# A Conformer layer's shifted copies in another layout, and two modulation vectors made elsewhere

## The chip, the cores and the metric

The kernel runs on one NeuronCore of a Trainium2 chip. TensorE (PE in the profile) multiplies matrices into PSUM, VectorE (DVE) and ScalarE (ACT) work elementwise, GpSimd (POOL) and SyncE (SP) mostly issue DMAs, and 16 DMA engines serve the queues of the core. The metric is the device time of one execution in microseconds (us), the median over runs; lower is better.

## The reference

A backbone of four layers works on 256 latent tokens and 256 context tokens of width 1024, all in float32. Layers 0 and 3 mix tokens by attention, layer 1 by a Conformer convolution, layer 2 by a short convolution; each is followed by an MLP. Six modulation vectors for each layer (shift, scale and gate of the mixer, numbers 0 to 2, and of the MLP, 3 to 5) come from one product of a conditioning vector with `mod_w`, 1024 by 6144 for each layer.

```python
def conformer_conv(h, w1, b1, dw, dwb, ln_g, ln_b, w2, b2):
    a, g = jnp.split(h @ w1 + b1, 2, axis=-1)
    u = a * jax.nn.sigmoid(g)
    u = dwconv(u, dw) + dwb                      # 31 taps along the tokens, each channel by itself
    return jax.nn.silu(layernorm(u, ln_g, ln_b)) @ w2 + b2

mod_l = (silu_c @ mod_w[i] + mod_b[i]).reshape(b, N_MOD, 1, D_MODEL)      # mod_c the same, from c_ctx
x = x + mod_l[:, 2] * mixer(modulate(rmsnorm(x), mod_l[:, 0], mod_l[:, 1]))
x = x + mod_l[:, 5] * sq_relu_mlp(modulate(rmsnorm(x), mod_l[:, 3], mod_l[:, 4]))
```

## The kernel before

Channels lie on the 128 partitions, in eight tiles; both streams, latent and context, lie side by side along a tile, 512 columns. The big products split each float32 operand into a high and a low part and add three products (lines 105 to 107). A weight chunk comes by an SP load into one of four `raw` buffers, ScalarE rounds it (line 221), VectorE takes the rest (line 222), and the two parts fill two of ten `w` buffers. `gemm_turns` goes over a pair of chunks once for the latent stream and once more for the context stream, and holds the eight `w` buffers of the pair until the second turn is through.

A scheduler that is not part of the kernel orders the instructions of each engine, except that from the second group of the Conformer's first product on, TensorE keeps program order until the block `with in_order` ends. The SP queue works in order too: a DMA that waits holds up all behind it.

The Conformer (`conformer`) makes the gated product `glu` in four groups of two tiles. Tiles 0 and 1 are convolved on VectorE (`conv_vector`), tiles 2 to 7 on TensorE (`conv_tensor`): 31 taps are eight products, each of which takes four neighbouring taps at once, from copies that hold each of 32 channels four times on the partitions, shifted by 0, 8, 16 and 24 columns. `shifted` writes a tile's `glu` to DRAM (`mem`) and reads it back in four such copies (`u4`, shown as `u<-mem`). The first of the four shifts fills partitions 0 to 31, the second 32 to 63, and so on. Groups 1 and 2 (tiles 2 to 5) treat both streams at once, group 3 (tiles 6 and 7) one at a time. After group 3 TensorE runs `conv_tensor` of tiles 4 to 7 for the latent stream, the mean of the layer norm (`total` and four `conv` against `ones_d`, line 1044), the context half of tiles 4 and 5, sums of squares (line 490), tile 6, the spread of the result over the partitions (line 527), tile 7, and the context mean. Then come the context sums and spread, and the product with `cv_w2` (`project`), whose operand `z` is ready by stream.

A modulation vector is made in one of two ways. `mod_tensor` loads its 4 MB in eight `raw` buffers and uses TensorE (16 products, line 371, and four small ones, line 380). `mod_vectors` loads 256 KB pieces into four buffers of their own (`mraw`) and uses VectorE (lines 312 and 316, then 322 and 323). Both are generators, put in a list by `background`; `tick`, called at steps of the big products, advances the first one at the rate given, and `need` runs the list at once until a vector is there.

Layer 1's vectors 0 to 3 are made by `mod_vectors` in layer 0's MLP, 4 and 5 by `mod_tensor` at rate 0, so that `self.need(layer, 4, 5)` at the end of the block `with in_order` runs both there, on TensorE between the context mean and the context sums.

Of the kernel before, what the change touches and what calls it, by code (L numbers as in the profile page):

```python
# [8 lines left out]
F32 = mybir.dt.float32  # L9
# [16 lines left out]
CONF_K = 31  # L26
CONF_PAD = 15
PITCH = 288
VECTOR_TILES = (0, 1)
NEG = -1e30  # L30


class Net:
# [864 lines left out]
    def conv_taps(self, slot):  # L898


        nc = self.nc
        dw = self.t["cv_dw"][slot]
        src = self.tmp([P, 2, P])
        nc.gpsimd.memset(src[96:, 1, 96:], 0.0)
        for b in range(2):
            for i in range(4):
                n = 3 if 4 * b + i == 7 else 4
                nc.gpsimd.dma_start(out=src[32 * i:32 * i + 32, b, :32 * n], in_=bass.AP(
                    dw.tensor, dw.offset + (4 * b + i) * D, [[32, 32], [8 * D, n], [1, 32]]))
        yield  # L910
        taps = self.work.tile([P, 8, 32], F32, tag="acc", bufs=1, name=self.name("taps"))
        ps = self.ps("x")
        for b in range(2):
            nc.tensor.transpose(out=ps[:, b * P:(b + 1) * P], in_=src[:, b], identity=self.ident)
        nc.vector.tensor_copy(out=taps, in_=ps[:, :2 * P].rearrange("p (i q) -> p i q", q=32))
        yield taps, self.mask32

    def conformer(self, layer, slot, then):
        nc, t = self.nc, self.t
# [3 lines left out]
        conv = [None] * KT  # L923
        sig = {}
        two = lambda ap: ap.rearrange("p (s n) -> p s n", s=2)
# [26 lines left out]
                        [P, 4, 4, 32]), op=ALU.mult)  # L952
            return halves

        def shifted(j, st):


            if j not in u4:
                u4[j] = [self.work.tile([P, 2, LAT + 8], F32, tag="h", bufs=22, name=self.name("u4")) for _ in range(4)]
                mem[j] = self.dram.tile([P, 2, PITCH], F32, tag=f"mem{j}", name=self.name("mem"))  # L960
            nc.sync.dma_start(out=mem[j][:, st], in_=glu[j][:, st])
            n = len(range(2)[st])
            for q in range(4):
                src = mem[j][32 * q:32 * q + 32, st]
                nc.sync.dma_start(out=u4[j][q][:, st, :LAT + 7], in_=bass.AP(
                    src.tensor, src.offset, [[8, 4], [2 * PITCH, 32], [PITCH, n], [1, LAT + 7]]))

        def conv_tensor(j, st):

            n = len(range(2)[st]) * LAT  # L970
            ps = self.ps()
            out = ps[:, :n].rearrange("p (s n) -> p s n", n=LAT)
            for i in range(8):
                for q in range(4):
                    nc.tensor.matmul(out=out[32 * q:32 * q + 32], lhsT=tapw[j][i // 4][:, i % 4, q],  # L975
                                     rhs=u4[j][q][:, st, i:i + LAT], start=i == 0, stop=i == 7, tile_position=(0, 32 * q))
            nc.scalar.activation(out=two(conv[j])[:, st], in_=out, func=AF.Identity, bias=self.par("cv_dwb", j))
# [9 lines left out]
        u4, tapw, mem = {}, {}, {}  # L987
        glu = {}
        for g in range(4):
            def out(d, src, c, g=g):  # L990
                j = 2 * g + d % 2
                if d < 2:
                    if j not in sig:
                        sig[j] = self.tmp()
                    nc.scalar.activation(out=sig[j][:, c], in_=src, func=AF.Sigmoid, bias=self.par("cv_b1", KT + j))
                    return
                if j not in glu:
                    glu[j] = self.padded(j, CONF_PAD)
                for s in range(c.start // LAT, c.stop // LAT):
                    o = s * LAT - c.start  # L1000
                    nc.vector.scalar_tensor_tensor(out=glu[j][:, s, CONF_PAD:CONF_PAD + LAT], in0=src[:, o:o + LAT],
                                                   scalar=self.par("cv_b1", j), in1=sig[j][:, s * LAT:(s + 1) * LAT],
                                                   op0=ALU.add, op1=ALU.mult)
                if j not in VECTOR_TILES:
                    shifted(j, slice(c.start // LAT, c.stop // LAT))
                elif c.stop == NTOK:
                    conv[j] = self.hid()
                    on_vector.append(conv_vector(j, glu[j]))
                    next(on_vector[-1])
            segs = [(D + g * LAT, LAT), (g * LAT, LAT)]  # L1010
            if g == 0:
                self.gemm_turns(self.chunk_pair(w1, segs), acts, out, first=True)
                in_order.enter_context(self.tc.manual_schedule(engines={mybir.EngineType.PE}))
            elif g < 3:
                for i, _ in enumerate(self.gemm(w1, segs, acts, cols, out)):
                    run_some(3)
                    if g == 1 and i == 1:
                        taps, mask = next(loaded)
                    if g == 2 and i in (2, 4):
                        tapw[1 + i // 2] = tap_weights(1 + i // 2)  # L1020
            else:
                for j in (2, 3):
                    conv[j] = self.hid()
                    conv_tensor(j, slice(0, 2))
                self.gemm_turns(self.chunk_pair(w1, segs), acts, out)
                for j in (4, 5, 6, 7):
                    tapw[j] = tap_weights(j)
# [31 lines left out]

        with in_order:  # L1060
            for j in (4, 5, 6, 7):
                conv_tensor(j, slice(0, 1))
            lat = layer_norm(0)
            next(lat)
            for j in (4, 5):
                conv_tensor(j, slice(1, 2))
            next(lat)
            conv_tensor(6, slice(1, 2))
            next(lat)
            conv_tensor(7, slice(1, 2))  # L1070
            other = layer_norm(1)
            next(other)
            self.need(layer, 4, 5)
        for _ in other:
            pass
        self.need(layer, 2)
# [194 lines left out]
    def run(self, out):  # L1271
        self.begin()
        for m in (2, 3, 4, 5):
            self.background(self.mod_tensor, 0, [m], 0.5)
        self.credit = -1.0
        both, lat = (0, NTOK), (0, LAT)
        for layer in range(DEPTH):
            slot = layer // 3
            live = both if layer < DEPTH - 1 else lat
            mixer_end = lambda s, layer=layer: self.norm(layer, 1, s)  # L1280
            if layer == DEPTH - 1:
                mixer_end = self.last_norm
            if layer % 3 == 0:
                self.attention(layer, slot, live, mixer_end)
            elif layer == 1:
                self.conformer(layer, slot, mixer_end)
            else:
                self.short_conv(layer, slot, mixer_end)
            if layer < DEPTH - 1:
                for vectors, rate in (([0, 1], 0.55), ([2, 3], 0.55)) if layer == 0 else (([0, 1], 0.42), ([2], 0.42), ([3, 4], 0.42),  # L1290
                                                                                   ([5], 0.25)):
                    self.background(self.mod_vectors, layer + 1, vectors, rate)
                if layer == 0:
                    for m in (4, 5):
                        self.background(self.mod_tensor, 1, [m], 0.0)

                def layer_end(s, layer=layer):
                    self.norm(layer + 1, 0, s)
                self.mlp(layer, live, layer_end)
            else:  # L1300
                self.mlp(layer, live, lambda s: None)
        self.end(out)
# [35 lines left out]
```

## Time and profile before

| | |
|---|---|
| median of 3 runs | 2233.25 us (2231.36 to 2234.01) |
| profiled execution, its own time | 2232.96 us |
| its span, first to last instruction | 2231.2 us |
| TensorE busy in the span | 2188.0 us, 98% |
| VectorE busy | 1522.8 us, 68% |
| ScalarE busy | 865.7 us, 39% |
| mean granted clock of TensorE | 0.99 |

The rows further down come from the profiled execution. Times count from the start of the span. A granted clock of 1.00 is 2.4 GHz, 0.50 is 1.2 GHz, and a value between the two is a mean over a stretch that had both. A float32 product of the convolution or of the modulation stands as two records, one of the big products as one, and a few per cent of the records are missing.

### The profile page before, as it was taken

To read this page: it belongs to the slowest core of one execution; us is meant where nothing else is said; L and a number is where in the kernel's file an instruction comes from. 1 tells how busy PE (TensorE), PEld (TensorE's weight loads), DVE (VectorE), ACT (ScalarE), POOL (GpSimd) and SP (SyncE) were. 2 spreads that over 40 slices of the span, in tenths; PEclk is the share of its full clock that TensorE was granted. 3 is DMA by queue.
4 is the path that set the end of the run, shared out by engine and by line. 5 is a ranking of instruction groups with operands and counts; after the bars stand their busy time and mean duration, and the time that the engine had idled before them with its cause. 6 is when DMAs were issued, how large, how long until landed. Compare 5 with 4: busy or idle time off the path is not lost.

```text
span 2231.2 us, 32928 instructions
## 1 busy us (share of the span) xinstructions
PE 2188.0 (98%) x12804; PEld 1792.8 (80%) x12804; DVE 1522.8 (68%) x2656; ACT 865.7 (39%) x1453; POOL 94.7 (4%) x167
## 2 busy tenths in 40 slices
PE   8999999999999988999999999999999999999998
PEld 5767678888889664988888898898888888778998
DVE  5366568979546835697766886579757566688665
ACT  4355545232234104542232332242323244666543
POOL 1112100000000000000000000000000000230000
PEclk9999999999999998999999999999999999999999
DMA  9555545646332336254545544226455426455553
GB/s 317 149 94 93 128 121 166 192 139 193 99 98 88 104 119 214 92 161 146 167 135 166 170 133 132 95 81 208 146 170 185 145 68 188 69 82 156 191 186 124
DMA packets 203132, 318.57 MB, mean 143 GB/s; under 512 B 13957, under 2 KB 70209, under 8 KB 202976
## 3 DMA queue, kind: packets, MB, share of 16 engines
q1 hardware_dynamic: 199056, 309.75, 43.6%
q0 software_dynamic: 3616, 6.60, 4.9%
q8 instruction: 100, 1.64, 0.3%
q14 instruction: 56, 0.46, 0.1%
q10 hardware_dynamic: 304, 0.12, 0.0%
HBM read 313.60 MB, written 2.82 MB: 142 GB/s over the span
## 4 chain that ended last, share of the span: by engine, by line
PE 91%; DMA 4%; DVE 3%; issue 1%; ACT 1%; POOL 0%; SPq 0%; ACTq 0%; POOLq 0%; DVEq 0%
PE mm L105 27%; PE mm L107 27%; PE mm L106 27%; PE mm L745 2%; PE x L735 2%; DMA u<-mem 2%; PE mm L707 1%; PE mm L975 1%; PE x L371 1%; PE mm L706 1%; DMA e<-in_na_rpb_dram 1%; DMA raw<-in_mod_w_dram 0%; DVE w L222 0%; DMA raw<-in_mlp_w_dram 0%; PE x L270 0%
## 5 line engine op out<-in xcount | busy, mean ns | idle before, releaser
L221 ACT ACTIVATE w<-raw 128x1024 fp32r<-128x1024 f32 (+1 forms) x377 | 392.2, 1054 | 652.8 <-PE mm L106 559.2
L222 DVE TENSOR_TENSOR w<-raw,w 128x1024 fp32r<-128x1024 f32 (+1 forms) x377 | 454.3, 1221 | 270.5 <-ACT w L221 267.4
L105 PE MATMUL mm<-a,w 128*128 128x512 f32 (+2 forms) x1792 | 629.8, 352 | 2.3 <-DVE t L629 1.4
L106 PE MATMUL mm<-a,w 128*128 128x512 f32 (+2 forms) x1792 | 627.4, 351 | 0.0
L107 PE MATMUL mm<-a,w 128*128 128x512 f32 (+2 forms) x1792 | 625.0, 350 | 0.3 <-DVE w L222 0.3
L106 PE MATMUL mm<-h,w 128*128 128x256 f32 (+1 forms) x1504 | 507.3, 337 | 0.1
L105 PE MATMUL mm<-h,w 128*128 128x512 f32 (+1 forms) x1376 | 472.7, 344 | 0.1
L107 PE MATMUL mm<-h,w 128*128 128x512 f32 (+1 forms) x1376 | 471.1, 342 | 0.0
L105 PEld LDWEIGHTS mm<-a,w 128*128 128x128 f32 x1792 | 337.5, 189 | 53.3 <-issue 5.7
L107 PEld LDWEIGHTS mm<-a,w 128*128 128x128 f32 x1792 | 337.9, 189 | 48.0 <-DVE w L222 0.9
L106 PEld LDWEIGHTS mm<-a,w 128*128 128x128 f32 x1792 | 338.5, 189 | 45.5
L106 PEld LDWEIGHTS mm<-h,w 128*128 128x128 f32 x1504 | 284.4, 189 | 32.3 <-DVE h L222 0.5
L105 PEld LDWEIGHTS mm<-h,w 128*128 128x128 f32 x1376 | 259.3, 188 | 36.2 <-issue 3.9
L107 PEld LDWEIGHTS mm<-h,w 128*128 128x128 f32 x1376 | 259.1, 188 | 32.6 <-DVE mm L713 0.6
L316 DVE SCALAR_TENSOR_TENSOR macc<-mraw,cw,macc 128x512 f32<-128x512 f32 x392 | 272.7, 750 | 11.1 <-DMA mraw<-in_mod_w_dram 10.3
L588 DVE SCALAR_TENSOR_TENSOR x<-mm,mod,x 128x256 f32<-128x256 f32 x288 | 127.6, 480 | 93.4 <-PE mm L107 92.6
L221 ACT ACTIVATE h<-t 128x512 fp32r<-128x512 f32 (+1 forms) x148 | 80.7, 546 | 105.9 <-DVE t L619 89.3
L222 DVE TENSOR_TENSOR h<-t,h 128x512 fp32r<-128x512 f32 (+1 forms) x148 | 86.4, 585 | 28.9 <-ACT h L221 28.8
L618 ACT ACTIVATE t<-mm 128x512 f32<-128x512 f32 (+1 forms) x136 | 69.0, 509 | 94.0 <-PE mm L107 92.7
L619 DVE SCALAR_TENSOR_TENSOR t<-mm,t 128x512 f32<-128x512 f32 (+1 forms) x136 | 79.5, 587 | 37.1 <-ACT t L618 36.7
L556 ACT ACTIVATE a<-t,mod 128x256 fp32r<-128x256 f32 x120 | 53.4, 500 | 58.9 <-DVE t L543 58.9
L723 ACT ACTIVATE t<-mm,s 128x512 f32<-128x512 f32 (+1 forms) x96 | 58.9, 616 | 44.0 <-DVE s L721 43.2
(172 smaller groups left out, 1805.3 us busy)
## 6 DMA issues: line engine op xcount, KB each, us to landing
raw<-in_mlp_w_dram SPq DMA_DIRECT2D x256, 512.0 KB
mraw<-in_mod_w_dram SPq DMA_DIRECT2D x256, 256.0 KB
raw<-in_mod_w_dram SPq DMA_DIRECT2D x48, 512.0 KB
raw<-in_na_wqkv_dram SPq DMA_DIRECT2D x64, 256.0 KB
raw<-in_sc_win_dram SPq DMA_DIRECT2D x24, 512.0 KB
h<-in_mod_w_dram SPq DMA_DIRECT2D x32, 256.0 KB
raw<-in_na_wqkv_dram SPq DMA_DIRECT2D x16, 512.0 KB
raw<-in_na_wo_dram SPq DMA_DIRECT2D x16, 512.0 KB
```

The lines of the kernel that those rows point to most:

```text
L105: mm(out=out, lhsT=a[0], rhs=b[0], start=start, stop=False)
L106: mm(out=out, lhsT=a[0], rhs=b[1], start=False, stop=False)
L107: mm(out=out, lhsT=a[1], rhs=b[0], start=False, stop=stop)
L221: self.nc.scalar.activation(out=hi, in_=src, func=AF.Copy)
L222: self.nc.vector.tensor_tensor(out=lo, in0=src, in1=hi.bitcast(F32), op=ALU.subtract)
L316: nc.vector.scalar_tensor_tensor(out=acc[s], in0=raw, scalar=c, in1=acc[s], op0=ALU.mult, op1=ALU.add)
L556: self.nc.scalar.activation(out=hi[:, c], in_=t, func=AF.Identity, bias=sh)
L588: self.nc.vector.scalar_tensor_tensor(out=x, in0=src[:, o:o + LAT], scalar=self.mod1(layer, m, s, j), in1=x, op0=ALU.mult, op1=ALU.add)
L618: nc.scalar.activation(out=r, in_=src, func=AF.Relu)
L619: nc.vector.scalar_tensor_tensor(out=h, in0=src, scalar=0.0, in1=r, op0=ALU.max, op1=ALU.mult)
L723: nc.scalar.activation(out=soft[:, g], in_=s[:, g], func=AF.Exp, bias=nm[:, i:i + 1], accum_out=sm[:, i:i + 1])
L735: nc.tensor.transpose(out=tp[:, dst * P:(dst + 1) * P], in_=p[:, j * P:(j + 1) * P], identity=self.ident)
```

## The change

Four parts.

- The four shifts of a channel lie on neighbouring partitions (partition 4c + s instead of 32s + c), so that the read back from DRAM goes over 32 channels, then four shifts, then columns. The taps are put in the same order by one ScalarE copy ahead of their transpose, and the mask that picks them comes from one VectorE reduction instead of the constant `mask32`.
- For tiles with both streams (2 to 5), the streams lie in DRAM in one run, the left padding of the second being the right padding of the first, so that each partition reads one run of 534 columns instead of two of 263. It is written by two DMAs instead of one. Tiles 6 and 7 get a DRAM buffer for each stream instead of halves of one.
- `conv_tensor` takes one stream at a time everywhere: for tiles 2 and 3 that is 64 products of 256 columns each instead of 32 of 512.
- Layer 1's vector 4 is made by `mod_vectors` in layer 0's MLP (all at rate 0.5 there instead of 0.55), and vector 5 by `mod_tensor` at rate 0.45 in layer 1's own MLP. `self.need(layer, 4, 5)` goes.

```diff
+CLOSE = CONF_PAD + 256
...
+        turned = self.tmp([P, 2, P])
+        nc.scalar.copy(out=turned.rearrange("p b (c s) -> p b s c", s=4), in_=src.rearrange("p b (s c) -> p b s c", s=4))
...
+        mask = self.work.tile([P, 32], F32, tag="red", bufs=1, name=self.name("mask"))
+        nc.vector.tensor_reduce(out=mask, in_=self.ident.rearrange("p (c s) -> p c s", s=4), axis=AX.X, op=ALU.add)
...
-            nc.sync.dma_start(out=mem[j][:, st], in_=glu[j][:, st])
+            if c == slice(0, NTOK):
+                pitch, n = 2 * CLOSE + 18, CLOSE + LAT + 7
+                mem = self.dram.tile([P, pitch], F32, tag=f"mem{j}", name=self.name("mem"))
+                nc.sync.dma_start(out=mem[:, :CLOSE], in_=glu[j][:, 0, :CLOSE])
+                nc.sync.dma_start(out=mem[:, CLOSE:2 * CLOSE + 16], in_=glu[j][:, 1, :CLOSE + 16])
+            else:
+                pitch, n = PITCH, LAT + 7
+                mem = self.dram.tile([P, pitch], F32, tag=f"mem{j}{s}", name=self.name("mem"))
+                nc.sync.dma_start(out=mem, in_=glu[j][:, s])
             for q in range(4):
-                src = mem[j][32 * q:32 * q + 32, st]
-                nc.sync.dma_start(out=u4[j][q][:, st, :LAT + 7], in_=bass.AP(
-                    src.tensor, src.offset, [[8, 4], [2 * PITCH, 32], [PITCH, n], [1, LAT + 7]]))
+                src = mem[32 * q:32 * q + 32]
+                nc.sync.dma_start(out=u4[j][q][:, s * CLOSE:s * CLOSE + n],
+                                  in_=bass.AP(src.tensor, src.offset, [[pitch, 32], [8, 4], [1, n]]))
...
-                    conv_tensor(j, slice(0, 2))
+                    for s in range(2):
+                        conv_tensor(j, s)
...
-            self.need(layer, 4, 5)
...
-                for vectors, rate in (([0, 1], 0.55), ([2, 3], 0.55)) if layer == 0 else (([0, 1], 0.42), ([2], 0.42), ([3, 4], 0.42),
-                                                                                   ([5], 0.25)):
+                if layer == 1:
+                    self.background(self.mod_tensor, 1, [5], 0.45)
+                for vectors, rate in ((([0, 1], 0.5), ([2, 3], 0.5), ([4], 0.5)) if layer == 0 else
+                                      (([0, 1], 0.42), ([2], 0.42), ([3, 4], 0.42), ([5], 0.25))):
                     self.background(self.mod_vectors, layer + 1, vectors, rate)
-                if layer == 0:
-                    for m in (4, 5):
-                        self.background(self.mod_tensor, 1, [m], 0.0)
```

What the scheduler makes of it is seen in the order of the instructions. TensorE's queue at the end of the Conformer's convolution, before (`total` and `conv` are the operands of the context mean; `raw` and `cw` are modulation weights and the conditioning vectors; `acc` holds squares; `z` and `h` are the high and low parts of the operand of the `cv_w2` product):

```order
L1044 MATMUL mm_7811<-conv_7396,ones_d 128x256
L1044 MATMUL mm_7811<-conv_7397,ones_d 128x256
L371 MATMUL x_7847<-raw_7848,cw 32x512 x2
L371 MATMUL x_7847<-raw_7850,cw 32x512 x2
...
L380 MATMUL x_7882<-mask_78,t_7880 128x4 x4
L371 MATMUL x_7890<-raw_7891,cw 32x512 x2
...
L380 MATMUL x_7925<-mask_78,t_7923 128x4 x4
L490 MATMUL x_7933<-ones,acc_7430 128x1 x2
L105 MATMUL mm_8033<-z_7414,w_8010 128x256
```

And now, where lines stand one to twelve lower:

```order
L1056 MATMUL mm_7978<-conv_7563,ones_d 128x256
L1056 MATMUL mm_7978<-conv_7564,ones_d 128x256
L106 MATMUL mm_8115<-z_7581,w_8092 128x256
L107 MATMUL mm_8115<-h_7582,w_8092 128x256
...
L107 MATMUL mm_8122<-h_7592,w_8104 128x256
L491 MATMUL x_8015<-ones,acc_7597 128x1 x2
L108 MATMUL mm_8122<-z_7591,w_8105 128x256
...
L106 MATMUL mm_8115<-z_7595,w_8110 128x256
L528 MATMUL x_8036<-ident,s_8034 128x128 x2
```

The modulation products are gone from between the mean and the sums; 68 products with `cv_w2` stand there, 17 more between the sums and the spread, and 11 more of the latent turn after the spread (192 products make both turns of the first half).

SP's queue from the `glu` of tile 4 on, before (`mem` the DRAM buffer, `u` on its right `glu`, on its left the shifted copies):

```order
L961 DMA mem_6999<-u_6990 128x576
L965 DMA u_1395_6995<-mem_6999 128x2x263
...
L961 DMA mem_7029<-u_7020 128x576
L360 DMA raw_7848<-in_mod_w_dram 128x2x512
L360 DMA raw_7850<-in_mod_w_dram 128x2x512
L965 DMA u_1401_7025<-mem_7029 128x2x263
...
L360 DMA raw_7856<-in_mod_w_dram 128x2x512
L360 DMA raw_7858<-in_mod_w_dram 128x2x512
L961 DMA mem_7246<-u_7238 128x288
L961 DMA mem_7260<-u_7252 128x288
L965 DMA u_1427_7242<-mem_7246 128x1x263
```

And now:

```order
L969 DMA mem_7094<-u_7085 128x271
L970 DMA mem_7094<-u_7085 128x287
L977 DMA u_1423_7090<-mem_7094 128x1x534
...
L95 DMA raw_8091<-in_cv_w_dram 128x2x512
L95 DMA raw_8097<-in_cv_w_dram 128x2x512
L977 DMA u_1429_7121<-mem_7125 128x1x534
...
L95 DMA raw_8103<-in_cv_w_dram 128x2x512
L95 DMA raw_8109<-in_cv_w_dram 128x2x512
L95 DMA raw_8355<-in_cv_w_dram 128x2x512
L974 DMA mem_7411<-u_7403 128x288
L974 DMA mem_7425<-u_7417 128x288
```

Loads of `cv_w2` stand where loads of `mod_w` stood; the twelve remaining `mod_w` loads before, which stood behind the last `u<-mem` and ahead of all of `cv_w2`, are gone from there.

TensorE's queue early in layer 1's MLP now (`a` is the MLP's input); before, no row of line 371 stands there:

```order
L108 MATMUL mm_8720<-a_8538,w_8709 128x256
L528 MATMUL x_8778<-ident,s_8774 128x128 x2
L372 MATMUL x_8837<-raw_8838,cw 32x512 x2
L372 MATMUL x_8837<-raw_8840,cw 32x512 x2
L106 MATMUL mm_8713<-a_8540,w_8708 128x256
...
L372 MATMUL x_8837<-raw_8927,cw 32x512
L372 MATMUL x_8837<-raw_8929,cw 32x512 x2
```

Vector 5's 16 products come in four groups between products of the MLP, and its eight loads stand on SP among the MLP's weight loads.

## Rows read from the trace of the kernel before

**Rows 1.** The page: span, and busy time, share and instructions by engine.

```profile
span 2231.2 us, 32928 instructions
...
PE 2188.0 (98%) x12804; PEld 1792.8 (80%) x12804; DVE 1522.8 (68%) x2656; ACT 865.7 (39%) x1453; POOL 94.7 (4%) x167
```

**Rows 2.** Waits of TensorE, 760 to 890 us: total us, times, longest us.

```profile
PE mm L975 <- DMA u<-mem: 7.8, 7, 2.8
```

**Rows 3.** Busy us by stretch; then clock, DMA engines' busy share, GB/s.

```profile
752.00:766.00 14.00, 14.00 (x62) 11.31 (x62) 14.00 (x21) 2.32 (x3) 0.00 (x0) 1.00 0.27 93
...
784.58:807.14 22.56, 22.56 (x193) 22.43 (x193) 13.97 (x23) 2.37 (x5) 0.00 (x0) 1.00 0.45 132
807.14:834.42 27.28, 20.06 (x258) 9.70 (x257) 0.88 (x2) 1.42 (x3) 0.00 (x0) 0.87 0.40 121
...
854.55:881.76 27.21, 19.58 (x82) 4.36 (x82) 7.94 (x25) 7.60 (x18) 0.00 (x0) 0.75 0.84 273
881.76:934.04 52.28, 49.54 (x401) 49.15 (x401) 34.26 (x78) 31.82 (x59) 1.23 (x14) 0.93 0.37 121
380.00:560.00 180.00, 180.00 (x785) 146.02 (x784) 158.81 (x240) 53.53 (x66) 0.00 (x0) 1.00 0.55 174
560.00:680.00 120.00, 120.00 (x540) 98.00 (x539) 58.34 (x84) 38.49 (x49) 0.00 (x0) 1.00 0.31 97
```

**Rows 4.** The chain that ended last, 764 to 890 us: start us, us, what.

```profile
777.51 7.06 PE mm L975 x58
...
800.61 13.34 DMA u<-mem
...
836.77 7.06 PE mm L975 x128
...
868.88 6.97 DMA raw<-in_mod_w_dram
...
883.89 1.24 DVE w L222
...
885.97 0.85 PE x L527 x4
```

**Rows 5.** SP's timeline: start us, us, line, DMA, count issued in a row.

```profile
749.79 17.40 SPq L965 DMA_DIRECT2D u<-mem  x8
...
797.92 6.20 SPq L965 DMA_DIRECT2D u<-mem  x4
804.21 3.37 SPq L360 DMA_DIRECT2D raw<-in_mod_w_dram  x2
807.68 1.08 SPq L961 DMA_DIRECT2D mem<-u  x2
817.03 6.49 SPq L965 DMA_DIRECT2D u<-mem  x8
```

**Rows 6.** TensorE by line, 300 to 360 us: records | busy us, mean ns.

```profile
L371 PE MATMUL x<-raw,cw 128*32 128x512 f32 x32 | 4.3, 605 | 0.0
...
L380 PE MATMUL x<-mask,t 128*128 128x4 f32 x8 | 0.9, 242 | 0.0
```

**Rows 7.** Timelines of TensorE and VectorE: start us, us, instruction.

```profile
843.76 0.61 PE L490 MATMUL x<-ones,acc 128*128 128x1 f32 x4
...
847.89 0.71 PE L527 MATMUL x<-ident,s 128*128 128x128 f32 x4
...
846.37 0.16 DVE L519 SCALAR_TENSOR_TENSOR s<-s,s 128x2 f32<-128x2 f32 x1
...
854.16 0.42 DVE L222 TENSOR_TENSOR h<-t,z 128x256 fp32r<-128x256 f32 x1
...
934.04 0.28 PE L105 MATMUL mm<-a,w 128*128 128x256 f32 x1
```

**Rows 8.** VectorE by line, 380 to 560 us: records | busy us, mean ns.

```profile
L316 DVE SCALAR_TENSOR_TENSOR macc<-mraw,cw,macc 128x512 f32<-128x512 f32 x97 | 65.9, 749 | 0.0
...
L322 DVE STREAM_TRANSPOSE t<-macc 128x512 f32<-128x512 f32 x14 | 9.2, 691 | 0.0
```

More of the change, by code (lines that the diff above doesn't have):

```diff
@@ L913, in conv_taps @@
         for b in range(2):
-            nc.tensor.transpose(out=ps[:, b * P:(b + 1) * P], in_=src[:, b], identity=self.ident)
+            nc.tensor.transpose(out=ps[:, b * P:(b + 1) * P], in_=turned[:, b], identity=self.ident)
         nc.vector.tensor_copy(out=taps, in_=ps[:, :2 * P].rearrange("p (i q) -> p i q", q=32))
-        yield taps, self.mask32
+        mask = self.work.tile([P, 32], F32, tag="red", bufs=1, name=self.name("mask"))
+        nc.vector.tensor_reduce(out=mask, in_=self.ident.rearrange("p (c s) -> p c s", s=4), axis=AX.X, op=ALU.add)
+        yield taps, mask
     def conformer(self, layer, slot, then):
@@ L953, in tap_weights, with shifted @@
             return halves
-        def shifted(j, st):
+        def shifted(j, c):
             if j not in u4:
-                u4[j] = [self.work.tile([P, 2, LAT + 8], F32, tag="h", bufs=22, name=self.name("u4")) for _ in range(4)]
-                mem[j] = self.dram.tile([P, 2, PITCH], F32, tag=f"mem{j}", name=self.name("mem"))
-            nc.sync.dma_start(out=mem[j][:, st], in_=glu[j][:, st])
-            n = len(range(2)[st])
-            for q in range(4):
-                src = mem[j][32 * q:32 * q + 32, st]
-                nc.sync.dma_start(out=u4[j][q][:, st, :LAT + 7], in_=bass.AP(
-                    src.tensor, src.offset, [[8, 4], [2 * PITCH, 32], [PITCH, n], [1, LAT + 7]]))
@@ L968, in conv_tensor @@
-        def conv_tensor(j, st):
-            n = len(range(2)[st]) * LAT
+                u4[j] = [self.work.tile([P, CLOSE + LAT + 7], F32, tag="h", bufs=22, name=self.name("u4")) for _ in range(4)]
+            s = c.start // LAT
+            if c == slice(0, NTOK):
[7 more added lines that the diff above has]
+                nc.sync.dma_start(out=mem, in_=glu[j][:, s])
@@ L971, in conv_tensor @@
+            for q in range(4):
+                src = mem[32 * q:32 * q + 32]
+                nc.sync.dma_start(out=u4[j][q][:, s * CLOSE:s * CLOSE + n],
+                                  in_=bass.AP(src.tensor, src.offset, [[pitch, 32], [8, 4], [1, n]]))
+        def conv_tensor(j, s):
             ps = self.ps()
-            out = ps[:, :n].rearrange("p (s n) -> p s n", n=LAT)
             for i in range(8):
                 for q in range(4):
-                    nc.tensor.matmul(out=out[32 * q:32 * q + 32], lhsT=tapw[j][i // 4][:, i % 4, q],
-                                     rhs=u4[j][q][:, st, i:i + LAT], start=i == 0, stop=i == 7, tile_position=(0, 32 * q))
@@ L977, in conv_tensor @@
-            nc.scalar.activation(out=two(conv[j])[:, st], in_=out, func=AF.Identity, bias=self.par("cv_dwb", j))
+                    nc.tensor.matmul(out=ps[32 * q:32 * q + 32, :LAT], lhsT=tapw[j][i // 4][:, i % 4, q],
+                                     rhs=u4[j][q][:, s * CLOSE + i:s * CLOSE + i + LAT], start=i == 0, stop=i == 7,
+                                     tile_position=(0, 32 * q))
+            nc.scalar.activation(out=two(conv[j])[:, s], in_=ps[:, :LAT], func=AF.Identity, bias=self.par("cv_dwb", j))
@@ L985, in run_some @@
                     n -= 1
-        u4, tapw, mem = {}, {}, {}
+        u4, tapw = {}, {}
         glu = {}
@@ L1004, in out @@
                 if j not in VECTOR_TILES:
-                    shifted(j, slice(c.start // LAT, c.stop // LAT))
+                    shifted(j, c)
                 elif c.stop == NTOK:
@@ L1061, in conformer @@
             for j in (4, 5, 6, 7):
-                conv_tensor(j, slice(0, 1))
+                conv_tensor(j, 0)
             lat = layer_norm(0)
@@ L1065, in conformer @@
             for j in (4, 5):
-                conv_tensor(j, slice(1, 2))
+                conv_tensor(j, 1)
             next(lat)
-            conv_tensor(6, slice(1, 2))
+            conv_tensor(6, 1)
             next(lat)
-            conv_tensor(7, slice(1, 2))
+            conv_tensor(7, 1)
             other = layer_norm(1)
             next(other)
-            self.need(layer, 4, 5)
         for _ in other:
```

## The prediction, made before the changed kernel had run

> **What bounds the kernel now.** I read the page first: TensorE is busy for 2188.0 of 2231.2 us [rows 1]. Only time that TensorE gives back can shorten the run, so I looked for its waits, and for work on it that a wait elsewhere stretches. In the list of waits, one stretch stands out, 760 to 890 us, the end of the Conformer: there the products of line 975 wait 7.8 us for the shifted copies [rows 2]. The busy share hides more than that list shows. I therefore read the stretches one by one, with the granted clock. The latent convolution of tiles 4 to 7 takes 27.28 us at a clock of 0.87, while the two context convolutions right after it, the same kind and size of work, take 7.06 us for two tiles, so 14.1 us would do for four [rows 3, 4]. Next, the two modulation vectors hold TensorE for 27.21 us at a clock of 0.75, with the DMA engines 0.84 busy [rows 3]; made in the middle of a long run of big products, one vector takes 4.3 + 0.9 us [rows 6]. Here the reader is to see that a busy TensorE is not one at its pace: both stretches are paced by DMAs, and the clock falls in them.
>
> The chain of waits names the DMAs: a copy issued at 800.61 ends 13.34 us later, and a load of `mod_w` issued at 868.88 ends 6.97 us later [rows 4]. SP's timeline says why the copies are late. Eight of them hold the queue for 17.40 us, and in 752 to 766 us, when hardly anything but copies is in flight, the DMA engines are 0.27 busy and move 93 GB/s [rows 3, 5]. A copy's outermost dimension is the four shifts, and 0.27 is about four engines of sixteen. The latent `mem<-u` of tiles 6 and 7 is issued at 807.68, behind tile 5's copies (797.92) and two `mod_w` loads (804.21), and its own copies only at 817.03, when TensorE is already there [rows 5].
>
> **The change, part by part.**
>
> *The copies.* A copy of 128 runs of 534 columns moves 273 KB. The stretch of the `mod_w` loads moved 273 GB/s, which gives 1.0 us for one; from above, it stays at the 17.40/8 = 2.2 us of now [rows 3, 5]. Its runs are as long as those of the weight loads (2 KB) and it now has 32 channels outermost, not four shifts, so I take 1.0 us. Tile 5's copies then land while group 3's products run (784.58 to 807.14 [rows 3]), the latent `mem<-u` of tiles 6 and 7 goes out soon after its `glu`, in the middle of that stretch, and the context buffers, being separate, need not wait until the latent copies are read. All copies are there before TensorE asks, and the latent convolution takes 14.1 us: **-13.2 us**. The lower end is 0, if the copies stay as slow. The extra DMA for each two-stream tile costs SP about 0.5 us (two `mem<-u` in 1.08 [rows 5]), under group 2's and 3's products; were that cover gone, 2 us for four tiles. SP's new order puts three `cv_w2` loads ahead of the latent `mem<-u`. The third needs a `raw` buffer that is freed by a split on VectorE ahead of group 3's `glu`, so it doesn't hold `mem<-u` past its data.
>
> The Trainium skill, "DMA: Bandwidth & Descriptors", section "Why a DMA increments its semaphore by 16 and not by 1", says that a DMA uses the largest number of engines, up to 16, that divides the outermost dimension of both sides. By it the copies go from 4 engines to 16 and the term is -13.2, where the rows alone leave it between -13.2 and 0; the trace agrees for the 4 (0.27 of 16).
>
> *Smaller products.* Tiles 2 and 3: 64 products of 256 columns instead of 32 of 512. One tile takes 7.06 us in the wide form and two half tiles take 7.06 us in the narrow form [rows 4], so 0. The ScalarE copy of the taps, 256 columns, and the VectorE mask are each of the size of a 0.42 us piece [rows 7] and come under groups 0 and 1; on the path they would cost 0.8.
>
> *Vectors 4 and 5 out of the tail.* From the end of the context mean (854.55) to the MLP's first product (934.04) there are 27.21 + 52.28 = 79.5 us [rows 3, 7]. What remains of it: 384 products with `cv_w2`, at group 3's 22.56 us for 192 [rows 3], 45.1 us. Two pairs of sums and spreads, 0.61 + 0.71 each [rows 7], 2.6 us. And what of the context layer norm now lies bare. VectorE has 7.9 us of work from the mean to the last square, nearly all that it does in 854.55 to 881.76 [rows 3]; 68 products of 8.0 us cover it. From the sums (843.76 + 0.61 = 844.37) to the scale (846.37 + 0.16 = 846.53) it took 2.2 us for the latent stream [rows 7]; 17 products of 2.0 us cover it but for 0.2. From the spread (847.89 + 0.71 = 848.60) to the fourth `z` (854.16 + 0.42 = 854.58) it took 6.0 us [rows 7], and the second turn's first column needs four `z`. Eleven products of the first turn (1.3 us) and nine that need only three `z` (1.1) lie beside it, so 3.6 us are bare. Bounds: 0, if `z` comes faster than TensorE uses it, and 6.0. Sum 45.1 + 2.6 + 0.2 + 3.6 = 51.5, so **-28.0 us**. `cv_w2` is split early, since its loads take the queue places and `raw` buffers of `mod_w`; the wait for a split at 883.89 [rows 4] goes.
>
> *Vector 5 in layer 1's MLP.* TensorE is the bound there, so it pays in full: 4.3 + 0.9 [rows 6], **+5.2 us**. Its eight loads share the four `raw` buffers and the SP queue with the MLP's weights. They add 4.2 MB over about 30 us of products, 140 GB/s on top of the 174 GB/s of an MLP stretch like 380 to 560; the 273 GB/s of now in the tail shows that much is possible only nearly, but the first loads go ahead of time. I take no wait, and keep it as a rival.
>
> *Vector 4 on VectorE in layer 0's MLP.* Two halves, each at most 16 first or further products (0.749) and two transposes and two reductions (0.69 or less): 2 x (12.0 + 2.8) = 29.5 us [rows 8]. They follow vectors 0 to 3, so they land in 560 to 680 us, where VectorE has 120 - 58.3 = 61.7 us free; in 380 to 560 it is 88% busy with no gap on TensorE, and the rate falls there from 0.55 to 0.5 [rows 3]. Cost 0; without the cover, up to 29.5. On TensorE it adds four products with few columns, at most the 0.9 us of line 380 [rows 6]: **+0.9 us**. Layer 2's vectors come some 16 steps later and fit into its short convolution.
>
> **Sum.** -13.2 - 28.0 + 5.2 + 0.9 = -35.1. From the profiled execution's 2232.96 that is 2197.9; the median of the runs is 0.3 above that execution, so I predict **2198 us**.
>
> **The rivals.**
>
> *The copies stay slow* (few engines, or the latency of writing to DRAM and reading back rules). For it: each copy waits for its write, and 807.68 to 817.03 is 9.35 us for that, though behind a full queue [rows 5]. Against it: 0.27 of the engines is a matter of spread, not of latency. Then the first term is 0: 2198 + 13 = 2211 us.
>
> *The tail lies bare.* The modulation products, slow as they were, covered the context layer norm. If the `cv_w2` products can't start (a split late, as at 883.89), TensorE waits from the end of the squares to `z`. Now it takes 886.82 - 881.76 = 5.1 us from the last modulation product to the end of the spread (885.97 + 0.85 [rows 4]), and 6.0 us more to the fourth `z`: 11.1 instead of my 0.6 + 0.2 + 0.7 + 3.6 = 5.1, so 6.0 more. A waiting TensorE also loses clock, 0.93 over 52.28 us [rows 3], 3.7 us. Result 2198 + 9.7 = 2208 us. The Trainium skill, "TensorE: Matmul & The Clock Gate", section "HAM oscillation — how this bites in real kernels", says that waits for DMAs between stretches of products bring the clock down, so that the next stretch starts cold, which speaks against taking out work that fills a wait; the trace agrees with 0.87 and 0.75. Against this rival: VectorE and ScalarE have room to split `cv_w2` during group 3 and the latent convolution (0.88 us of VectorE in 27.28 [rows 3]).
>
> *Vector 5 starves layer 1's MLP.* Four `raw` buffers serve both. If loads land late as in the tail, each costs up to 6.97 us [rows 4]. One or two waits give 2204 to 2212. This is the case that can end on the other side: six such loads (four groups and two pairs of weights behind them) are 41.8 us, 2240, slower than now; it decides from 35.1/6.97, five full waits. Against it: in the tail twelve loads stood in a row with nothing else to do, here products run between the groups.
>
> **How the numbers follow.** My case, 2192 (nothing bare, and small waits of now gone too) to 2204 (6.0 bare, some waiting): 0.67. Copies slow: 0.10. Tail bare: 0.08. MLP starved in part: 0.10; in full, slower: 0.03. Still faster, under 2190: 0.02. The range is 2190 to 2211 us and leaves out a little under 2 in 10. About 0.2%, 4.5 us, is what a measurement of this kernel can tell from no change. All cases but the starved one in full lie beyond that: faster 0.95, same 0.02, slower 0.03.
>
> **What would show it.** In the profile after: the copies' stretch with the DMA engines well above 0.27; no wait of the convolution for `u<-mem`; latent convolution in about 14 us at a clock of 1.00; no products of line 371 (now 372) before the MLP, and about 51 us from the context mean to the MLP; a bare wait of 3 to 4 us ahead of the second turn; vector 5 in four groups of about 1 us each in layer 1's MLP with no wait for `raw` beside them; VectorE fuller in 560 to 680 us with TensorE still without a gap. I am wrong if the copies' share stays near 0.27, if MLP products wait for `w`, or if the tail still takes over 60 us.

## The result, and the profile after

The changed kernel takes 2198.89 us (median of 4 runs, 2196.46 to 2200.30) against 2233.63 us before (4 runs, 2231.36 to 2236.13): a ratio of 0.9843, with a 95% interval of 0.9832 to 0.9855. The gain is 34.7 us; the forecast was 2198.

The page of the kernel after, beside [rows 1]:

```profile
span 2196.9 us, 33176 instructions
...
PE 2168.3 (99%) x12900; PEld 1791.8 (82%) x12900; DVE 1543.7 (70%) x2697; ACT 868.1 (40%) x1455; POOL 94.6 (4%) x167
```

TensorE is busy 19.7 us less and idle 14.6 us less, although its work is nearly the same. The stretches say where; here the kernel after, with the columns of [rows 3] (busy PE, PEld, DVE, ACT, POOL; clock, DMA share, GB/s):

```profile
752.00:756.00 4.00, 4.00 (x19) 3.22 (x19) 4.00 (x7) 1.06 (x1) 0.00 (x0) 1.00 0.91 283
770.41:784.51 14.10, 14.10 (x258) 8.94 (x257) 14.10 (x21) 2.15 (x4) 0.00 (x0) 1.00 0.79 251
784.44:807.11 22.67, 22.67 (x200) 22.54 (x200) 10.70 (x16) 4.94 (x8) 0.00 (x0) 1.00 0.49 159
807.04:821.08 14.04, 14.04 (x258) 8.12 (x257) 3.14 (x4) 2.72 (x5) 0.00 (x0) 1.00 0.67 210
...
841.20:890.16 48.96, 47.99 (x401) 47.26 (x400) 35.75 (x92) 32.40 (x70) 1.23 (x14) 1.00 0.18 55
890.16:1248.30 358.14, 358.04 (x1732) 293.26 (x1730) 262.31 (x414) 115.25 (x162) 0.24 (x3) 1.00 0.49 155
...
347.27:692.38 345.11, 345.11 (x1646) 285.04 (x1645) 272.69 (x428) 108.63 (x149) 0.00 (x0) 1.00 0.49 152
```

And three stretches of the kernel before that [rows 3] doesn't hold: tiles 2 and 3, layer 1's MLP from its first product to its latent sums of squares, and layer 0's MLP likewise from the spread ahead of it:

```profile
769.10:784.58 15.48, 14.93 (x130) 4.15 (x129) 7.56 (x11) 2.69 (x3) 0.00 (x0) 1.00 0.49 131
...
934.04:1285.68 351.64, 350.39 (x1683) 290.83 (x1682) 277.99 (x437) 113.59 (x161) 0.23 (x3) 1.00 0.49 154
...
346.90:691.04 344.14, 344.14 (x1638) 285.41 (x1637) 248.26 (x384) 108.86 (x149) 0.00 (x0) 1.00 0.45 141
```

The reader is to put like beside like. Copies' stretch, from about 2 us after the first of the eight is issued until SP turns to weight loads: DMA share 0.27, now 0.91. Tiles 2 and 3: 15.48, now 14.10. Group 3: 22.56, now 22.67. Latent convolution: 27.28 at a clock of 0.87, now 14.04 at 1.00. Context mean to the MLP's first product: 27.21 + 52.28 = 79.5 at 0.75 and 0.93, now 48.96 at 1.00. Then some is given back: layer 1's MLP 351.64, now 358.14; layer 0's MLP 344.14, now 345.11.

SP's timeline after, beside [rows 5]:

```profile
750.87 5.12 SPq L977 DMA_DIRECT2D u<-mem  x8
...
796.57 0.82 SPq L974 DMA_DIRECT2D mem<-u  x2
798.39 5.53 SPq L977 DMA_DIRECT2D u<-mem  x8
```

Eight copies hold SP for 5.12 us instead of 17.40, and the latent `mem<-u` of tiles 6 and 7 goes out at 796.57 instead of 807.68, its copies at 798.39 instead of 817.03, ahead of TensorE's need at 807.04.

TensorE's waits after, 745 to 890 us, beside [rows 2]: no copy and no `raw` is among them, and the three waits sum to 0.8 us.

```profile
PE x L491 <- DVE acc L480: 0.3, 1, 0.3
PE mm L106 <- ACT z L222: 0.3, 1, 0.3
PE x L528 <- DVE s L520: 0.2, 1, 0.2
```

Behind the Conformer two waits are new, both from VectorE, 1200 to 1500 us, where the kernel before has none:

```profile
PE mm L108 <- DVE w L223: 2.0, 2, 1.5
PE x L330 <- DVE red L324: 0.8, 1, 0.8
```

### The profile page after: what moved, and what is told of

It is laid out like the page before. It is cut to its first block, busy times and chain, and to the rows that moved or that the text cites. A ratio compares the mean times of both kernels' runs of the same rounds, so it can differ in the third digit from the quotient of the medians.

```text
span 2196.9 us, 33176 instructions
## 1 busy us (share of the span) xinstructions
PE 2168.3 (99%) x12900; PEld 1791.8 (82%) x12900; DVE 1543.7 (70%) x2697; ACT 868.1 (40%) x1455; POOL 94.6 (4%) x167
## 4 chain that ended last, share of the span: by engine, by line
PE 94%; DVE 3%; DMA 2%; issue 1%; ACT 1%; POOL 0%; ACTq 0%; POOLq 0%; DVEq 0%; SPq 0%
PE mm L106 28%; PE mm L108 28%; PE mm L107 28%; PE mm L985 2%; PE x L736 2%; PE mm L746 2%; PE mm L708 1%; PE x L372 1%; PE mm L707 1%; DMA e<-in_na_rpb_dram 1%; PE x L491 0%; DMA raw<-in_mlp_w_dram 0%; DVE a L558 0%; DVE w L223 0%; PE x L271 0%
## 5 line engine op out<-in xcount | busy, mean ns | idle before, releaser
L317 DVE SCALAR_TENSOR_TENSOR macc<-mraw,cw,macc 128x512 f32<-128x512 f32 x420 | 292.7, 745 | 12.3 <-DMA mraw<-in_mod_w_dram 11.0
L724 ACT ACTIVATE t<-mm,s 128x512 f32<-128x512 f32 (+1 forms) x96 | 59.0, 617 | 45.1 <-DVE s L722 44.3
```

The lines of the kernel that those rows point to most:

```text
L317: nc.vector.scalar_tensor_tensor(out=acc[s], in0=raw, scalar=c, in1=acc[s], op0=ALU.mult, op1=ALU.add)
L724: nc.scalar.activation(out=soft[:, g], in_=s[:, g], func=AF.Exp, bias=nm[:, i:i + 1], accum_out=sm[:, i:i + 1])
```

## The experiments

**The two parts apart.** The copies alone (`copies_only`) are the changed kernel with these lines; the vectors alone (`vectors_only`) are the kernel before with the same lines the other way round:

```diff
             next(other)
+            self.need(layer, 4, 5)
...
-                if layer == 1:
-                    self.background(self.mod_tensor, 1, [5], 0.45)
-                for vectors, rate in ((([0, 1], 0.5), ([2, 3], 0.5), ([4], 0.5)) if layer == 0 else
-                                      (([0, 1], 0.42), ([2], 0.42), ([3, 4], 0.42), ([5], 0.25))):
+                for vectors, rate in (([0, 1], 0.55), ([2, 3], 0.55)) if layer == 0 else (([0, 1], 0.42), ([2], 0.42), ([3, 4], 0.42),
+                                                                                   ([5], 0.25)):
                     self.background(self.mod_vectors, layer + 1, vectors, rate)
+                if layer == 0:
+                    for m in (4, 5):
+                        self.background(self.mod_tensor, 1, [m], 0.0)
```

> The changed copies, taps and buffers, with the modulation vectors 4 and 5 made where they were before (on TensorE between the context mean and the context sums). Theory: the two parts of the change add up, and the copies alone are worth what the trace after shows between 706 us and the context mean, 14.7 us: 2233.6 - 14.7 = about 2219 us, with the latent convolution at 14.0 us, a stretch of copies with the DMA engines over 0.8 busy, and a tail (context mean to the MLP's first product) that stays at 79 us. Rival: the time goes over into the tail, because the loads for the two vectors have 14 us less of a head start: the tail grows to some 90 us and the time is 2229 to 2233 us.

> The old copies, with vectors 4 and 5 made where the change makes them. Theory: the tail is worth 30.6 us, vector 5 costs 5.9 in layer 1's MLP, vector 4 costs 1.0 in layer 0's, and layers 2 and 3 lose some 3.7: 2233.6 - 20.0 = about 2213.6 us, with the waits for the shifted copies still there and the latent convolution at 27 us. Rival: the slow copies hold up the loads of cv_w2 on SP's queue, so that the tail is bare or waits for a split: the tail stays over 60 us and the time is 2225 us or more.

The copies alone give 2218.84 us (0.9932, 0.9915 to 0.9949), as the theory had it. The vectors alone give 2217.98 us (0.9929, 0.9914 to 0.9944), 4.4 us above it, and yet not by its rival. Windows of the copies alone (copies, latent convolution, modulation products, the rest up to the MLP):

```profile
752.85:756.85 4.00, 4.00 (x19) 3.26 (x18) 4.00 (x7) 1.07 (x1) 0.00 (x0) 1.00 0.88 267
807.99:822.02 14.03, 14.03 (x258) 8.11 (x257) 0.88 (x2) 1.42 (x3) 0.00 (x0) 1.00 0.33 100
842.15:866.52 24.37, 16.29 (x73) 3.14 (x73) 7.88 (x24) 6.66 (x18) 0.00 (x0) 0.93 0.87 299
866.52:919.60 53.08, 50.82 (x409) 50.35 (x409) 34.25 (x78) 32.71 (x60) 1.23 (x14) 0.94 0.38 121
```

and of the vectors alone (copies, latent convolution, tail):

```profile
751.00:766.00 15.00, 15.00 (x67) 12.12 (x66) 15.00 (x23) 2.13 (x3) 0.00 (x0) 1.00 0.33 109
808.33:840.62 32.29, 21.68 (x258) 9.84 (x257) 5.18 (x6) 5.00 (x8) 0.00 (x0) 0.84 0.60 162
862.36:910.80 48.44, 47.56 (x400) 47.00 (x400) 35.12 (x91) 31.80 (x69) 1.15 (x14) 1.00 0.19 55
```

With the copies alone the tail stays long, 24.37 + 53.08 = 77.5 us, its first part still paced by the loads (0.87). With the vectors alone the tail is short, 48.44. So the tail answers to the vectors, and the convolution at full pace needs the fast copies. The gains apart are 14.8 + 15.7 = 30.5 us, and together 34.7. By the times alone this difference isn't clear of noise, since the intervals allow 11.4 to 19.0 and 12.5 to 19.2 us for the parts. The profiled executions show where it would come from: with the slow copies and the early `cv_w2` loads in one stretch the DMA share there rises from 0.40 to 0.60 and the convolution takes 32.29 us, 5.0 more than before. Taking the vectors out of the tail moves loads forward into the copies' stretch, and only fast copies leave room for them; that reading rests on these rows of one execution each and wasn't tried by itself.

**What makes a copy fast.** First the old order of dimensions, with the old taps and mask, on the new runs and buffers (`shifts_outer`), then the new order with runs half as long (`two_copies`):

```diff
-                                  in_=bass.AP(src.tensor, src.offset, [[pitch, 32], [8, 4], [1, n]]))
+                                  in_=bass.AP(src.tensor, src.offset, [[8, 4], [pitch, 32], [1, n]]))
```

```diff
-                nc.sync.dma_start(out=u4[j][q][:, s * CLOSE:s * CLOSE + n],
-                                  in_=bass.AP(src.tensor, src.offset, [[pitch, 32], [8, 4], [1, n]]))
+                for b in (range(2) if c == slice(0, NTOK) else (s,)):
+                    nc.sync.dma_start(out=u4[j][q][:, b * CLOSE:b * CLOSE + LAT + 7],
+                                      in_=bass.AP(src.tensor, src.offset + (b - s) * CLOSE, [[pitch, 32], [8, 4], [1, LAT + 7]]))
```

> The changed kernel, but a copy goes over the four shifts first and then over 32 channels, as before, with the old taps and mask; the single run of 534 columns, the separate buffers and the place of the vectors stay. Theory: the number of outermost steps sets how many DMA engines work, so the copies' stretch falls back to about 0.27 busy, a copy takes 2.2 us or more, TensorE waits for copies again and the time is 2198.9 + 13 to 15 = about 2213 us. Rival: it is the run length, the buffers and the earlier write that made the copies fast; then a copy still takes about 1 us and the time is 2199 us.

> The changed kernel, but the copy of a tile with both streams is cut in two DMAs, one for each stream, each with runs of 263 columns (1 KB) instead of 534 (2 KB), 32 channels still outermost. Theory: spread over the engines decides and run length doesn't; twice as many issues (16 of about 0.55 us for tiles 2 and 3, 8.8 us) still end before TensorE asks at 770 us, so the time is 2199 us (2197 to 2202) with no wait for a copy. Rival: run length made the gain; then the share falls to about half, copies come late and the time is 2205 to 2213 us.

Shifts outermost: 2218.83 us (0.9935, 0.992 to 0.995), as slow as the old copies with the same vectors (2217.98). Channels outermost in half runs: 2201.41 us (0.9852, 0.9837 to 0.9867). The copies' stretch of the one and of the other:

```profile
752.00:765.00 13.00, 13.00 (x58) 10.49 (x57) 13.00 (x19) 1.75 (x2) 0.00 (x0) 1.00 0.31 112
```

```profile
751.13:761.41 10.28, 10.28 (x46) 8.25 (x46) 10.28 (x16) 1.07 (x1) 0.00 (x0) 1.00 0.74 217
```

The order of the dimensions alone takes the share from 0.91 to 0.31. Half runs take it to 0.74, with 16 issues in 10.28 us on SP, and no wait for a copy appears. The 0.74 need not come from the shorter runs: SP takes 0.64 us for an issue in both kernels (10.28/16 and 5.12/8), and 128 runs of 263 columns, 135 KB, in each 0.64 us are 210 GB/s by this estimate, close to the 217 in the row. No run tells the two apart. As to the time, the 2.5 us in the medians can't be told from the scatter, since the intervals overlap. The single run and the separate buffers alone give nothing that the times show. The expectation for the first was 2213 us: 5.8 us are missing from it. TensorE's waits there, 760 to 880 us, and ScalarE's timeline:

```profile
PE mm L981 <- DMA u<-mem: 6.6, 7, 2.1
PE mm L106 <- ACT h L984: 5.2, 1, 5.2
```

```profile
801.29 1.06 ACT L222 ACTIVATE w<-raw 128x1024 fp32r<-128x1024 f32 x1 [16.85 <-DMA raw<-in_cv_w_dram]
```

The 5.2 us are a wait of group 3's products. The view names an activation of line 984, but ScalarE had stood idle for 16.85 us until a weight load landed, and that activation came behind the rounding of those weights. So slow copies can also delay the weight loads among them.

The Trainium skill, "DMA: Bandwidth & Descriptors", section "Why a DMA increments its semaphore by 16 and not by 1", has a DMA take the largest number of engines up to 16 that divides the slowest dimension of both sides: 4 for the shifts, 16 for the 32 channels. The shares 0.31 and 0.91 agree. Which engines were at work no row here shows.

**What makes the tail short.** Program order kept through the `cv_w2` product, so that none of its products may pass the context sums and spread (`bare_tail`: all that stands from the block's end to the line shown moves into the block); and vector 5 put back (`one_in_tail`):

```diff
-        self.project(t["cv_w2"][slot], z, cols, evac, then, first=True)
+            self.project(t["cv_w2"][slot], z, cols, evac, then, first=True)
```

```diff
             next(other)
+            self.need(layer, 5)
...
-                if layer == 1:
-                    self.background(self.mod_tensor, 1, [5], 0.45)
...
+                if layer == 0:
+                    self.background(self.mod_tensor, 1, [5], 0.0)
```

> The changed kernel, but TensorE keeps program order through the whole product with cv_w2, so that the context sums and spread stand ahead of all of its products. It tests whether the tail is short because products with cv_w2 lie beside the context layer norm. Theory (they are the cover): TensorE waits bare about 8 us for the squares of the context stream and 2.2 us for the scale, the latent turn then covers the rest: 2198.9 + 10 = about 2209 us. Rival (the tail is short only because the loads of the two vectors are gone, whatever lies beside the layer norm): 2199 us.

> The changed kernel with vector 5 made on TensorE between the context mean and the context sums, as before, instead of in layer 1's MLP; vector 4 stays on VectorE. Theory: a vector in the tail is paced by its loads and takes about 12 us there (24.4 us for two with the new copies), against 5.9 in the MLP, it delays the loads of cv_w2 behind its own, and the 2.2 us that layer 2's late vectors cost come back: 2198.9 + 12 - 5.9 - 2.2 + 0 to 5 = about 2205 us (2202 to 2208). Rival: the time for which it waits lies beside the layer norm anyway, and it costs no more than in the MLP: 2197 to 2199 us.

Program order: 2210.46 us (0.9899, 0.9884 to 0.9914), 11.6 above the changed kernel. One vector in the tail: 2205.46 us (0.9875, 0.986 to 0.989), 6.6 above it. Both are as the theory had them. The first one's waits, 838 to 900 us, and its tail:

```profile
PE x L491 <- DVE acc L480: 8.8, 2, 8.1
PE x L528 <- DVE s L520: 2.3, 1, 2.3
PE x L528 <- DVE s L506: 1.4, 1, 1.4
```

```profile
841.27:903.41 62.14, 49.63 (x400) 49.37 (x401) 38.87 (x98) 35.08 (x73) 1.22 (x14) 0.92 0.12 35
```

With hardly any DMA traffic (0.12) the tail is 62.14 us long instead of 48.96. So its length isn't settled by the loads of the vectors alone; what lies beside the layer norm counts. Not all of the 13.2 us belongs to it: the order is kept to the end of the product, and of the waits 0.7 (the second of line 491) and 1.4 us (line 506) stand there, where the changed kernel waits 0.3. The other's tail, and its waits, 838 to 900 us:

```profile
843.05:906.70 63.65, 56.81 (x441) 50.72 (x441) 41.70 (x99) 38.77 (x76) 1.22 (x14) 0.95 0.46 150
```

```profile
PE x L372 <- DMA raw<-in_mod_w_dram: 3.2, 1, 3.2
PE mm L108 <- DVE w L223: 2.4, 1, 2.4
...
```

One vector lengthens the tail by 14.7 us, by its own products, its late loads, the split that waits behind them and a clock of 0.95. In the MLP it cost about 6, and the late vectors of layer 2 up to 2.8 more: 14.7 - 6.2 - 2.8 = 5.7 of the 6.6 us measured. That is why it is better there.

The clock in the tail: 1.00 in the changed kernel and with the vectors alone, 0.92 to 0.95 in the three kernels of this section in which TensorE waits there for several us (`copies_only`, `bare_tail`, `one_in_tail`). The Trainium skill, "TensorE: Matmul & The Clock Gate", section "HAM oscillation — how this bites in real kernels", says that waits between stretches of products bring the clock down; the rows agree, and the rival built on it did not come, because TensorE waits only 0.8 us in this stretch.

**Vector 5 elsewhere.** On VectorE, with vector 4 in layer 0's MLP (`both_vector`), or in layer 1's (`vec5_vector_mlp1`):

```diff
-                if layer == 1:
-                    self.background(self.mod_tensor, 1, [5], 0.45)
-                for vectors, rate in ((([0, 1], 0.5), ([2, 3], 0.5), ([4], 0.5)) if layer == 0 else
+                for vectors, rate in ((([0, 1], 0.55), ([2, 3], 0.55), ([4, 5], 0.55)) if layer == 0 else
```

```diff
                 if layer == 1:
-                    self.background(self.mod_tensor, 1, [5], 0.45)
+                    self.background(self.mod_vectors, 1, [5], 0.45)
```

> The changed kernel with both vectors, 4 and 5, made on VectorE in layer 0's MLP, as a pair at rate 0.55, as are vectors 0 to 3; nothing of layer 1's vectors in layer 1's MLP. Theory: TensorE saves the 5.9 us of vector 5's products, layer 2's vectors keep their old steps and the waits of 0.8 and 1.5 us at 1443 and 1445 us go; VectorE has some 59 us free in 380 to 680 us and needs 29.5: 2198.9 - 5.9 - 2.2 = about 2191 us. Rival: VectorE becomes too full in layer 0's MLP, splits of weights come late and TensorE waits there: 2199 us or more.

> The changed kernel with vector 5 made on VectorE in layer 1's MLP, ahead of layer 2's vectors, instead of on TensorE there. Theory: TensorE saves 5.9 us less 1 us for the four small products; layer 2's vectors come later still on VectorE, by up to 29.5 us of its work, and cost 1 to 4 us in the short convolution: 2195 to 2198 us. Rival: VectorE is full enough there that layer 2's vectors are late by much more, or vector 5 itself is late for the end of the MLP: 2202 us or more.

> The changed kernel once more, unaltered, beside the next one. Expected: 2199 us (2196.5 to 2201), a ratio of 0.984 to 0.985 to the kernel before.

> The version with vectors 4 and 5 both on VectorE in layer 0's MLP, once more, unaltered. If its gain over the changed kernel is real it stands 7 to 10 us below it again, at 2188 to 2192 us, a ratio of 0.980 to 0.981 to the kernel before, and the intervals of the two don't overlap; if not, both lie within 3 us of each other.

Both on VectorE in layer 0: 2189.65 us (0.9806, 0.9791 to 0.9821), and once more 2191.06 us (0.9819, 0.9804 to 0.9834) beside the changed kernel's 2198.73 us (0.9854, 0.9838 to 0.9871). The intervals of that pair don't overlap: this version beats the changed kernel by about 8 us (the second ratio, 0.9819, is a little above the 0.980 to 0.981 expected). VectorE in layer 0's MLP, and layer 1's MLP, in it:

```profile
380.00:560.00 180.00, 180.00 (x786) 145.68 (x785) 158.76 (x241) 53.17 (x65) 0.00 (x0) 1.00 0.56 176
560.00:680.00 120.00, 120.00 (x526) 96.96 (x525) 103.25 (x158) 37.46 (x48) 0.00 (x0) 1.00 0.54 166
...
892.31:1244.27 351.96, 350.72 (x1682) 290.32 (x1681) 278.01 (x437) 113.86 (x161) 0.24 (x3) 1.00 0.49 154
```

TensorE has no gap in either stretch of layer 0, at 158.76 of 180 and 103.25 of 120 us of VectorE. Layer 1's MLP is back at 351.96 us, so vector 5 had cost it 358.14 - 351.96 = 6.2. The two waits of 1200 to 1500 us are gone. 6.2 + 2.8 is the 8 to 9 us.

In layer 1's MLP: 2197.95 us (0.984, 0.9824 to 0.9857), no different from the changed kernel. Most of what TensorE saves it loses to a split, in its waits of 940 to 990 us:

```profile
PE mm L108 <- DVE w L223: 4.0, 1, 4.0
```

and the waits for layer 2's late vectors stay. The expected range took these in only by its upper end.

## Why the prediction was right, point by point

*Copies, -13.2.* Right in place and kind. The latent convolution fell from 27.28 to 14.04 us, which is -13.2, and tiles 2 and 3 gave another 1.4 that the sum left at nothing: 0.55 of it is a wait for a copy that is gone, 15.48 - 14.93. The other 0.83 stands in the rows as busy time; see the next point. A copy of 273 KB at the 283 GB/s of the copies' stretch is 1.0 us, as assumed. The rival of slow copies fell: `shifts_outer` is what it looks like, at 2218.8.

*Smaller products, 0.* Not refuted, but read from a row that doesn't carry it: the 7.06 us of [rows 4] hold 58 records, and a wide tile of 32 products has 64. In the kernel before TensorE has 14.93 us of work for tiles 2 and 3, now 14.10. With narrow products behind slow copies, in `shifts_outer`, it is 14.42 without a wait:

```profile
771.75 14.42 PE L981 MATMUL mm<-u,tapw 128*32 128x256 f32 x256
```

So narrow products cost nothing against the wide ones as they ran. Whether the wide form or the late copies stretched the 14.93 is open: wide products with fast copies were not run.

*Tail, -28.0.* Right in kind, 2.5 us too small: 48.96 instead of 51.5. The step that failed is "So 3.6 us are bare". TensorE's timeline at the spread:

```profile
852.24 0.68 PE L528 MATMUL x<-ident,s 128*128 128x128 f32 x4 [0.19 <-DVE s L520]
...
854.54 0.51 PE L106 MATMUL mm<-z,w 128*128 128x256 f32 x2 [0.32 <-ACT z L222]
```

The 0.2 ahead of the spread came out as 0.19; the 3.6 behind it as 0.32. Two things made it smaller. First, the 6.0 us from the spread to the fourth `z` were read from the latent stream, where ScalarE loads a function table ahead of the first `z`; the context stream comes after it and needs no load:

```profile
849.26 1.28 ACT L1056 ACT_TABLE_LOAD   x1 [0.76 <-DVE t L1054]
```

```profile
857.07 0.42 DVE L223 TENSOR_TENSOR h<-t,z 128x256 fp32r<-128x256 f32 x1
```

The first line is the kernel before, the second the end of the fourth `z` after: from the spread (852.24 + 0.68 = 852.92) to 857.49 it took 4.6 us, so 1.4 of the 3.6 us were never there, and the table load is 1.28 of them. Second, I counted only the rest of the first turn and nine products of the second as cover. The order of the program has more there (`mm_8235` and `mm_8260` belong to the second turn, `mm_8379` to the next pair of chunks, whose latent operand had long been ready):

```
L106 MATMUL mm_8235<-z_7581,w_8092 128x256
L106 MATMUL mm_8260<-z_7581,w_8092 128x256
L106 MATMUL mm_8379<-z_7581,w_8356 128x256
L107 MATMUL mm_8379<-h_7582,w_8356 128x256
L108 MATMUL mm_8379<-z_7581,w_8357 128x256
L106 MATMUL mm_8379<-z_7583,w_8356 128x256
```

Products of three outputs are mixed, so that each new `z` is used several times before the next is needed. `bare_tail` shows what the cover as a whole is worth: without it the tail is 13.2 us longer, some 2 of them at its end. The tail as a whole fell short of the sum by less than the 3.3 us of this step, since it is busy for 47.99 us where 45.1 + 2.6 = 47.7 were expected, and idle for 1.0 where 3.8 were.

*Vector 5 in layer 1's MLP, +5.2.* Right in kind, 1 us too small: 6.2 by the stretch against the version without it. Its products, 895 to 1180 us, by line:

```profile
L372 PE MATMUL x<-raw,cw 128*32 128x512 f32 x32 | 5.3, 605 | 0.0
...
L381 PE MATMUL x<-mask,t 128*128 128x4 f32 x8 | 1.0, 242 | 0.0
```

One record lasts 605 ns as in [rows 6], but the 32 stand in five pieces among the big products and overlap less: 5.3 us instead of 4.3. No load of `raw` was waited for, so the rival of a starved MLP fell.

*Vector 4, 0 and +0.9.* Right: layer 0's MLP is 1.0 us longer with no gap, and VectorE has 24.4 us more to do there (29.5 was the bound).

*"Layer 2's vectors come some 16 steps later and fit into its short convolution."* This is the other failure. They end so late that a reduction, then the weight splits behind it on VectorE, are waited for. VectorE's timeline there, beside TensorE's waits of 0.76 us up to 1442.89 and 1.48 us up to 1444.64:

```profile
1442.07 0.68 DVE L324 TENSOR_REDUCE red<-t 128x16 f32<-128x512 f32 x1
1442.66 0.48 DVE L589 SCALAR_TENSOR_TENSOR x<-mm,mod,x 128x256 f32<-128x256 f32 x1
1443.21 0.24 DVE L337 TENSOR_TENSOR mod<-x,params 128x8 f32<-128x8 f32 x2
1443.37 1.22 DVE L223 TENSOR_TENSOR w<-raw,w 128x1024 fp32r<-128x1024 f32 x1
```

With 0.5 us at 1263 that is 2.8 us that the sum had at nothing.

Together: -13.2 - 1.4 (copies), -30.5 (tail), +6.2 (vector 5), +1.0 (vector 4), +2.8 (layer 2) = -35.1, against -34.7 measured. The mechanisms were right in the main, and the terms to 1 to 3 us. That the sum came out within 1 us of the forecast is luck: what was left out of it on one side (1.4 + 2.5) happens to balance what was left out on the other (1.0 + 2.8). The rival of the bare tail fell too: the split of `cv_w2` came in time, and the clock stayed at 1.00.

## What to carry to other kernels

A busy bottleneck engine can hide half its gain in stretches that run slow: divide the time of a stretch by that of the same work elsewhere in the trace, and look at the DMA share and the clock beside it. A DMA share that stays at a fraction such as 0.27 while one kind of copy is in flight asks for a look at the order of the copy's dimensions; longer runs alone left it at 0.31 here. Work that is taken from a wait is only free to go if something else covers the wait: look in the instruction order for what the scheduler can put there, from other outputs too, and follow what the moved work delays a layer later.

## What the runs showed of the hardware that was not expected

- Slow copies can delay more than their readers: with the shifts outermost ScalarE stood idle for 16.85 us until a weight load of another kind landed, and TensorE lost 5.2 us in a product that uses no copy.
- Halving the runs did little harm here: the same bytes in runs of 1 KB instead of 2 KB, by twice as many DMAs, moved 217 GB/s instead of 283, and no wait came of it. SP's 0.64 us for each issue is enough to explain the lower figure.
- A function table that one stream's layer norm loads on ScalarE can serve the next: in the changed kernel it is loaded at 835.85 us for the latent stream and not again ahead of the context activations at 853.53, and the context stream reached its fourth `z` 1.4 us sooner after its spread than the latent one in the kernel before, 1.28 of which are the load.
- What two parts of a change give apart may not add up: one moves loads into the stretch that the other makes fast. With the slow copies the DMA share there rose from 0.40 to 0.60 and the convolution took 5.0 us more; the gains themselves, 14.8 and 15.7 us apart and 34.7 together, differ by no more than their intervals allow.
